# Gates and values of three head groups by Strassen's seven half products, with the weight sums made by DMA in HBM and y kept in HBM

## The chip, the core and the metric

One core of a Trainium2 chip runs the whole program once. The time is device microseconds of that execution. Its engines work side by side, each with its own queue in strict order: TensorE (PE; PEld is its loading of stationary operands), VectorE (DVE), ScalarE (ACT), GpSimd (POOL) and SyncE (SP, which here only issues DMAs). ACT and POOL can issue DMAs too. Sixteen DMA engines carry all transfers.

## What is computed

Two layers over x of 512 positions and 1024 features, in float32. Layer 0 has eight heads of retention and an RG-LRU branch; layer 1 is differential attention. After each, h = LayerNorm(sqrt 2 * h + sublayer(h)). The change is in layer 1:

```python
def odd_layer(x, w_in, ..., subln_g, w_out, pos, lambda_init):
    proj = jnp.einsum('bsd,de->bse', x, w_in)          # 1024 -> q 2048, k 2048, v 2048, g 2048
    q, k, v, g = jnp.split(proj, ...)
    q = rope(q.reshape(B, S, 2 * DIFF_HEADS, DIFF_DH), pos) * (DIFF_DH ** -0.5)
    k = rope(k.reshape(B, S, 2 * DIFF_HEADS, DIFF_DH), pos)
    out = diff_attention(q, k, v.reshape(B, S, DIFF_HEADS, DIFF_DV), lam)   # w = softmax1 - lam * softmax2, w @ v
    out = out * lax.rsqrt(jnp.mean(jnp.square(out), axis=-1, keepdims=True) + NORM_EPS) * subln_g
    out = (out * (1.0 - lambda_init)).reshape(B, S, DIFF_WIDTH) * jax.nn.silu(g)
    return jnp.einsum('bse,ed->bsd', out, w_out)
```

## The kernel before

**Numbers.** Every float32 operand of a product is split into two float32r parts, a rounded high part (a cast on ScalarE) and the rest (a subtraction on VectorE), by `split`. `mm3` makes a product of three matmuls: high by high, high by low, low by high. h, the input of layer 1, lies in SBUF as such a pair, features on partitions, 8 k tiles of 128 by 512 positions.

**Weights.** They come in blocks of 128x1024 (0.5 MB), in the order of the list `order`. `fetch` issues the load on SP's queue into one of two raw buffers and splits it into one of five pairs (`wsp`); `take(n)` hands out the next pair and has n more fetched behind it. SP and PE keep the order of the program; the other engines' instructions are put in order when the program is built, by priority.

**Units of PE.** `t_unit` makes a head's q or k (one weight block, 8 k tiles, 24 matmuls). `s_unit` makes the gates or the values of a group of two heads: 512 columns, 4 blocks of 128 positions, 4 weight blocks, each used by 24 matmuls, 96 in all; four PSUM banks of the pool `ps_pj` hold the sums. `out_unit` multiplies the mixed heads by the output weights and adds the result to y with VectorE (L239), y being 4 blocks of 128x1024 in SBUF. Layer 1 has the groups 0 to 3 (od, L262): values and gates of group 0, q and k of heads 0 to 2, then for each group its gates, its values, the output unit of two finished heads and q and k of the next two; at the end heads 6 and 7 go out, and LayerNorm and the stores follow each row block.

**Side work.** Attention is written as generators, in steps (scores; softmax; transposes; values; norm; transposes), which `Side` puts between the matmuls of the units by counting ticks (one tick is three matmuls): a new block every 8 ticks, at most three at once. Its softmax and norm run on VectorE, ScalarE and, for the inverse root, POOL. `side.need` has a step's PE instructions written before a point; `past(i - 1)` has the attention of the group before finished before its gates and values are overwritten.

**Ends.** y starts as sqrt 2 * h: the first output unit of a layer scales it while adding (L237). In the last unit of layer 1, four weight blocks (w140 to w143) are fetched at its start, with nothing ahead of them on SP but the four loads of LayerNorm's parameters:

```python
odd_out((6, 7), "oo6", after=odd_end, late=P_LAST)      # the last output unit of layer 1
w = [take(1 if n == 2 else 0) for _ in range(n)]        # out_unit: its weights
```

Of the kernel before, what the change touches and what calls it, by code (L numbers as in the profile page):

```python
# [8 lines left out]
F32 = mybir.dt.float32  # L9
# [33 lines left out]
EARLY = 2  # L43

# [51 lines left out]
def trunk(ctx: ExitStack, tc: tile.TileContext, a):  # L96
# [15 lines left out]
    small = pool("small", 4)  # L112
    ps_pj = pool("ps_pj", 4, space=PS)
# [34 lines left out]
    def mm3(out, l, r, start, stop):  # L148
        nc.tensor.matmul(out=out, lhsT=l[0], rhs=r[0], start=start, stop=False)  # L149
        nc.tensor.matmul(out=out, lhsT=l[0], rhs=r[1], start=False, stop=False)  # L150
        nc.tensor.matmul(out=out, lhsT=l[1], rhs=r[0], start=False, stop=stop)  # L151
# [67 lines left out]
    def out_unit(mix, y, name, first, before=None, after=None, late=0):  # L219
        n = len(mix)  # L220
        w = [take(1 if n == 2 else 0) for _ in range(n)]
        for sb in range(SB):
# [10 lines left out]
            for hf, ps in enumerate(pss):  # L233
                yy = y[:, sb, hf * HALF:hf * HALF + HALF]
# [30 lines left out]
    for g in range(1, 4):  # L265
        od += [("g", g), ("v", g), *[("o", (2 * g - 2, 2 * g - 1))] * (g < 3), ("qk", 2 * g + 1), *[("qk", 2 * g + 2)] * (g < 3)]
    od.append(("o", (4, 5)))
    oi = 0
    for kind, i in od:
        if kind == "o":  # L270
            order += [(oo[2 * hd + j], j) for hd in i for j in range(2)]
        else:
            order += [(ow[oi + j], None) for j in range(4)]
            oi += 4
# [257 lines left out]

    for kind, i in ev:
# [34 lines left out]
    h = pair(big, [P, KT, S], "x", "h")  # L568

    def even_end(sb):  # L570
        pts = list(layer_norm(y, sb, gb0))

        def fin():
            for hf, hv in pts:
# [77 lines left out]
    def odd_out(hds, name, **kw):  # L652
# [5 lines left out]
        out_unit([t for hd in hds for t in mix_of(om[hd])], y, name, 0 in hds, before=before, **kw)  # L658
# [13 lines left out]
    for kind, i in od:  # L672
# [16 lines left out]
        elif kind == "g":  # L689
# [6 lines left out]
            s_unit(h, f"og{i}", False, evac)  # L696
        elif kind == "qk":
# [92 lines left out]
```

## Time and profile before

| | |
|---|---|
| median of 3 runs | 942.91 us (942.73 to 943.59) |
| the profiled execution | 943.21 us, its span 941.4 us |
| PE busy, PEld busy | 923.9 us (98%), 764.8 us (81%) |
| DVE, ACT, POOL busy | 692.7 us (74%), 463.6 us (49%), 58.6 us (6%) |
| moved by DMA | 88.95 MB, all issued by SP |
| gates and values of groups 1, 2, 3 | from 534.0, 660.0 and 791 us, with attention between, 54 to 58 us each |
| last output unit | 907.4 to 932.7 us |

A row of the profile's groups gives line, engine, operation, output and inputs, shapes, count, busy time and mean duration in ns, then the idle time before and what ended it. A row of the timeline begins with start and duration in us. Matmuls overlap their neighbours: the step from one to the next is shorter than the duration shown. A row on stretches has the busy time of each engine in that stretch. The page's chain of waits has PE for 64% of the span, DVE 19%, ACT 8%.

### The profile page before, as it was taken

The numbers are of one execution on the slowest core, as the hardware profiler recorded it, in microseconds if no ns is written. First come the engines' busy times: TensorE is split into PE (matmuls) and PEld (weight loads), VectorE is DVE, ScalarE is ACT, GpSimd is POOL, SyncE is SP. The second block draws the span as 40 slices with busy tenths as digits, with TensorE's granted clock in tenths as the row PEclk, the third lists the DMA queues.
The fourth block names the chain that finished last, engine by engine and source line by source line (L and its number), as shares of the span: only waits on it lengthen the run. The fifth ranks groups of instructions, "written<-read, shape, count | busy, mean of one in ns | idle before, by whom it ended". The sixth has DMA issues, their size and how long they took to land.

```text
span 941.4 us, 11566 instructions
## 1 busy us (share of the span) xinstructions
PE 923.9 (98%) x4327; PEld 764.8 (81%) x4327; DVE 692.7 (74%) x1171; ACT 463.6 (49%) x750; POOL 58.6 (6%) x118
## 2 busy tenths in 40 slices
PE   9999999999999999999999999999999999999996
PEld 7888888878887887888887888888788888887885
DVE  5877997868779988994489854478844488636777
ACT  5567786566374776423334454233453234444340
POOL 0000000000000000000001210100100001101023
PEclk9999999999999999999999999999999999999998
DMA  6562221512314123314221222042223142223102
GB/s 225 174 218 68 90 73 54 165 57 93 120 54 148 57 90 118 120 29 162 93 89 65 69 89 90 23 134 90 68 68 90 45 135 68 73 85 113 66 23 91
DMA packets 27418, 88.95 MB, mean 94 GB/s; under 512 B 3425, under 2 KB 3553, under 8 KB 27361
## 3 DMA queue, kind: packets, MB, share of 16 engines
q1 hardware_dynamic: 27360, 88.20, 28.6%
q8 instruction: 34, 0.56, 0.2%
q14 instruction: 24, 0.19, 0.1%
HBM read 86.09 MB, written 2.10 MB: 94 GB/s over the span
## 4 chain that ended last, share of the span: by engine, by line
PE 64%; DVE 19%; ACT 8%; issue 4%; DMA 2%; POOL 2%; SPq 0%; DVEq 0%; ACTq 0%; POOLq 0%
PE ov_ps L150 3%; PE ov_ps L151 3%; PE ov_ps L149 3%; PE og_ps L149 3%; PE og_ps L150 3%; PE og_ps L151 3%; PE ev_ps L149 2%; PE ev_ps L150 2%; PE oo_ps L149 2%; PE oo_ps L150 2%; PE oo_ps L151 2%; PE ev_ps L151 2%; ACT e L610 1%; PE xb_ps L149 1%; PE xb_ps L150 1%
## 5 line engine op out<-in xcount | busy, mean ns | idle before, releaser
L610 ACT ACTIVATE e<-as,nm 128x128 f32<-128x128 f32 (+3 forms) x64 | 33.2, 523 | 29.2 <-DVE nm L607 28.8
L641 DVE SCALAR_TENSOR_TENSOR o<-po,ars,og 128x256 f32<-128x256 f32 x32 | 15.5, 484 | 39.8 <-POOL ars L326 39.8
L607 DVE CUSTOM_DVE_ANT_0 as<-as,mask 128x128 f32<-128x128 f32 (+3 forms) x64 | 30.2, 510 | 1.9 <-PE as L151 1.9
L617 POOL TENSOR_SCALAR zr<-z 128x1 f32<-128x1 f32 x32 | 11.3, 352 | 309.9 <-ACT e L610 309.9
L325 POOL TENSOR_SCALAR rs_t<-bmv 128x1 f32<-128x1 f32 x6 | 2.3, 376 | 418.4 <-DVE bmv L336 418.4
L637 ACT ACTIVATE po<-po 128x256 f32<-128x256 f32 x32 | 11.8, 370 | 29.8 <-PE po L151 25.9
L325 POOL TENSOR_SCALAR rs_t<-ss,zr 128x1 f32<-128x1 f32 x32 | 16.0, 501 | 140.5 <-ACT po L637 135.5
L239 DVE TENSOR_TENSOR y<-oo_ps,y 128x512 f32<-128x512 f32 x24 | 16.3, 684 | 4.2 <-PE oo_ps L151 4.2
L326 POOL TENSOR_TENSOR ars<-rs_t,nhalf 128x1 f32<-128x1 f32 x32 | 18.9, 591 | 2.7
L482 DVE SCALAR_TENSOR_TENSOR xc<-xbp,vecs,xc 128x509 f32<-128x509 f32 (+2 forms) x24 | 17.9, 746 | 1.5 <-ACT xc L479 1.3
L618 DVE SCALAR_TENSOR_TENSOR e<-e,zr,e 128x128 f32<-128x128 f32 (+3 forms) x32 | 17.6, 551 | 1.0
L439 DVE TENSOR_TENSOR rsd<-rs,dec 128x512 f32<-128x512 f32 (+3 forms) x32 | 15.5, 486 | 1.1 <-PE rs L151 1.0
L615 DVE RECIPROCAL zr<-z 128x1 f32<-128x1 f32 x32 | 5.2, 162 | 15.1 <-ACT e L610 14.9
L646 PEld LDWEIGHTS po<-ident,o 128*128 128x128 f32 x64 | 8.3, 140 | 7.8 <-DVE o L641 4.8
L646 PE MATMUL po<-ident,o 128*128 128x128 f32 x64 | 12.6, 278 | 1.6 <-DVE o L641 1.4
L622 PE MATMUL wt<-ident,e 128*128 128x128 f32 x80 | 14.0, 272 | 0.0
L145 ACT CAST hh<-ht 128x512 fp32r<-128x512 f32 x8 | 4.7, 588 | 18.4 <-PE ht L577 18.4
L622 PEld LDWEIGHTS wt<-ident,e 128*128 128x128 f32 x80 | 10.4, 140 | 3.8 <-DVE e L618 0.4
L498 DVE TENSOR_TENSOR xbp<-xbp,xc 128x512 f32<-128x512 f32 x8 | 5.5, 690 | 9.9 <-ACT xbp L495 9.9
L610 ACT ACTIVATION_READ_ACCUMULATOR e<-as,nm 128x1 f32 x64 | 12.5, 196 | 0.0
L504 DVE SCALAR_TENSOR_TENSOR xc<-t,r 128x512 f32<-128x512 f32 x8 | 5.5, 691 | 9.0 <-ACT r L503 9.0
L408 ACT ACT_TABLE_LOAD x9 | 11.5, 1283 | 0.8 <-PE gl_ps L151 0.7
(2673 smaller groups left out, 3416.3 us busy)
## 6 DMA issues: line engine op xcount, KB each, us to landing
w_r<-in_od_w SPq DMA_DIRECT2D x64, 512.0 KB, 3.3
w_r<-in_ev_w SPq DMA_DIRECT2D x47, 512.0 KB, 3.3
w_r<-in_ev_wo SPq DMA_DIRECT2D x16, 512.0 KB, 3.4
w_r<-in_od_wo SPq DMA_DIRECT2D x16, 512.0 KB, 3.3
dec<-in_dec SPq DMA_DIRECT2D x8, 256.0 KB, 3.9
y<-in_x SPq DMA_DIRECT2D x4, 512.0 KB, 6.8
out_h<-y SPq DMA_DIRECT2D x8, 256.0 KB, 2.1
xr<-in_xt SPq DMA_DIRECT2D x3, 512.0 KB, 6.7
```

The lines of the kernel that those rows point to most:

```text
L149: nc.tensor.matmul(out=out, lhsT=l[0], rhs=r[0], start=start, stop=False)
L150: nc.tensor.matmul(out=out, lhsT=l[0], rhs=r[1], start=False, stop=False)
L151: nc.tensor.matmul(out=out, lhsT=l[1], rhs=r[0], start=False, stop=stop)
L239: nc.vector.tensor_tensor(out=yy, in0=ps, in1=yy, op=ALU.add)
L325: nc.gpsimd.tensor_scalar(out=t, in0=var, scalar1=scale, scalar2=eps, op0=ALU.mult, op1=ALU.add)
L326: nc.gpsimd.tensor_tensor(out=out, in0=t, in1=nhalf[:, :1], op=ALU.pow)
L482: nc.vector.scalar_tensor_tensor(out=xc[:, sh:], in0=xb[:, :S - sh], scalar=conv_w(w, c), in1=xc[:, sh:], op0=ALU.mult, op1=ALU.add)
L607: nc.vector.tensor_tensor_reduce(out=ps[:, :n], in0=ps[:, :n], in1=mask[:, S - n:], scale=-QK_SCALE, scalar=3.0e38, op0=ALU.add, op1=ALU.m ...
L610: nc.scalar.activation(out=e, in_=ps[:, :n], func=AF.Exp, scale=-1.0, bias=nm, accum_out=z[:, mp:mp + 1])
L618: nc.vector.scalar_tensor_tensor(out=ee[0], in0=ee[1], scalar=zr[:, 0:1], in1=ee[0], op0=ALU.mult, op1=ALU.add)
L622: nc.tensor.transpose(out=pt[:, kb * P:kb * P + P], in_=ee[0][:, kb * P:kb * P + P], identity=ident)
L646: nc.tensor.transpose(out=pm[:, i * P:i * P + P], in_=o[:, i * P:i * P + P], identity=ident)
```

## The change

1. **Gates and values of groups 1 to 3 are one unit, `gates_values`.** h is cut into halves of positions (r) and of features (c), the weights into two halves of features and gates against values. Seven products of such blocks replace eight: a product takes two weight blocks and makes two row blocks of 128x512 in 24 matmuls. Of the seven left factors three are plain blocks of h and four are sums; of the seven right ones three are plain weights and four are sums. Results are combined with copies on ScalarE and additions on VectorE; two pairs of `ps_pj` banks are used in turn. A weight block serves 12 matmuls, and a group takes 14 blocks where it took 8.
2. **The weight sums, `weight_sums`,** 24 blocks of 0.5 MB in HBM, are made by POOL's DMA queue: a copy from the weights and an accumulating transfer for each, 48 transfers of 0.5 MB. In the program they are side work from tick 30 on, 10 ticks apart.
3. **The sums of h, `act_sums`,** are made by VectorE behind the gates of group 0, in `st`, which takes y's place in SBUF; four pairs of 1 MB are stored to HBM by POOL's queue, and ACT's queue loads them into `sx` two at a time (`load_sum`, 2 DMAs of 0.5 MB each, eight per group).
4. **y in HBM.** After the even layer ScalarE scales h by sqrt 2 and POOL's queue stores it to `yd`. The first three output units copy their banks on ScalarE and POOL's queue adds them to `yd` (24 accumulating transfers of 256 KB). Before the last unit SP loads y again, 4 blocks of 0.5 MB.

```diff
+    sums = []
...
+        elif kind == "gv":
+            b = {(r, c): [ow[oi + 4 * c + 2 * r + j] for j in range(2)] for r in range(2) for c in range(2)}
+            t = {n: [dram.tile([P, D], F32, tag=f"t{i}{n}{j}", name=f"t{i}{n}{j}") for j in range(2)] for n in (1, 2, 3, 4)}
+            for j in range(2):
+                for n, one, two in ((1, b[0, 1], b[0, 0]), (3, b[1, 1], b[0, 1]), (2, b[1, 1], t[1]), (4, b[1, 0], t[2])):
+                    sums += [(t[n][j], one[j], None), (t[n][j], two[j], ALU.add)]
+            for n in (b[0, 0], b[1, 0], t[2], t[3], t[1], t[4], b[1, 1]):
+                order += [(n[j], None) for j in range(2)]
...
+    def weight_sums():
+        for dst, src, op in sums:
+            nc.gpsimd.dma_start(out=dst, in_=src, max_dma_last_dim=4 * D, **({"accum_op": op} if op else {}))
+            yield SUM_GAP
...
+    side.add(weight_sums(), "sums", 1, SUM_START)
...
+                nc.scalar.activation(out=hv, in_=hv, func=AF.Identity, scale=ALPHA)
+                nc.gpsimd.dma_start(out=yd[sb][:, hf * HALF:hf * HALF + HALF], in_=hv)
...
+    def add_to_y(sb, hf, ps):
+        t = work(f"oy{sb}{hf}")
+        nc.scalar.copy(out=t, in_=ps)
+        nc.gpsimd.dma_start(out=yd[sb][:, hf * HALF:hf * HALF + HALF], in_=t, accum_op=ALU.add)
...
+        def put(k, n):
+            split(lows[k], (st[:, k, 0].bitcast(F32R), st[:, k, 1].bitcast(F32R)))
+            nc.gpsimd.dma_start(out=sd[n], in_=st[:, k])
...
+        st = big.tile([P, 2, 2, KT // 2, 2 * P], F32, tag="y", name="st")
+        lows = [st[:, k, 1] for k in range(2)]
+        difference(lows[0], (1, 1), (1, 0))
+        add(lows[1], 0, 0, ALU.subtract, less(lows[1], lows[0]))
+        put(0, 0)
+        add(lows[0], 0, 1, ALU.subtract, less(lows[0], lows[1]))
+        put(1, 1)
+        put(0, 3)
+        difference(lows[1], (0, 0), (1, 0))
+        put(1, 2)
...
+    def load_sum(n, k):
+        for j in range(2):
+            nc.scalar.dma_start(out=sx[:, k, :, 2 * j:2 * j + 2].bitcast(F32), in_=sd[n][:, :, 2 * j:2 * j + 2])
...
+        def product(ps, left, start):
+            for j in range(2):
+                w = take(2)
+                for n in range(2):
+                    for kt in range(2 * j, 2 * j + 2):
+                        c = kt % 2 * HALF
+                        mm3(ps[n], left(kt, n), cut(w, ALL, slice(c, c + HALF)), start and kt == 0, kt == KT // 2 - 1, skip_group_check=not start)
+                        side.tick()
...
+        product(one, block(0, 0), True)
+        p1 = copies(one, "p1")
+        product(two, block(0, 1), True)
+        gate(two, p1, 0)
+        product(one, total(0), False)
+        u = copies(one, "u")
+        load_sum(0, 0)
+        product(two, total(1), True)
+        p7 = copies(two, "p7")
+        load_sum(3, 1)
+        product(one, total(0), False)
+        past(i - 1)
+        low = []
+        for n in range(2):
+            nc.vector.scalar_tensor_tensor(out=p7[n], in0=one[n], scalar=-1.0, in1=p7[n], op0=ALU.mult, op1=ALU.subtract)
+            low.append(pair(vp, [P, S], "v", f"ov{i}{2 + n}"))
+            split(p7[n], low[n])
+        product(two, block(1, 1), False)
+        gate(two, u, 1)
+        product(one, total(1), False)
...
-            odd_out(i, f"oo{i[0]}")
+            odd_out(i, f"oo{i[0]}", keep=add_to_y)
     gb1 = ln_params(a["od_ln"], "ln1", *((qkp, n) for n in ("qh", "ql", "kh", "kl")))
+    y = big.tile([P, SB, D], F32, tag="y", name="y2")
+    for sb in range(SB):
+        nc.sync.dma_start(out=y[:, sb], in_=yd[sb])
     odd_out((6, 7), "oo6", after=odd_end, late=P_LAST)
```

How the order of instructions changes, at three places. First POOL's queue at the start of the program. Before, the first instructions behind the memset are those of the LayerNorm after the even layer:

```order
L302 MEMSET nhalf_158 128x4
L325 ISA
L325 TENSOR_SCALAR rs_t_3412<-bmv_3409 128x1 [waits DVE_49]
L326 TENSOR_TENSOR lrs_3411<-rs_t_3412,nhalf_158 128x1 [waits Pool_49]
```

Now (t110 is a weight sum in HBM: group 1, sum 1, block 0; DMASW is a counter of landed POOL transfers):

```order
L320 MEMSET nhalf_184 128x4
L386 DMA t110_101<-in_od_w 128x1024
L386 DMA t130_105<-in_od_w 128x1024
L386 DMA t120_103<-in_od_w 128x1024
L386 DMA t110_101<-in_od_w 128x1024 [waits DMASW0_49]
L386 DMA t130_105<-in_od_w 128x1024 [waits DMASW1_49]
L386 DMA t140_107<-in_od_w 128x1024
L386 DMA t120_103<-t110_101 128x1024 [waits DMASW3_49,DMASW2_49]
L386 DMA t111_102<-in_od_w 128x1024
```

The 48 transfers stand in one row before LayerNorm's first instruction, and none of them waits for another engine: the ticks set their place in the order, nothing more. Second, VectorE in the gate stage of group 0 (ov02 and ov03 are values of group 0, which PE's banks hold until then; w68 to w71 the weights of that stage), before:

```order
L146 TENSOR_TENSOR w68l_3767<-w68_r_3765,w68h_3766 128x1024 [waits DMAHW6_49,Activation_49]
L146 TENSOR_TENSOR w69l_3773<-w69_r_3771,w69h_3772 128x1024 [waits DMAHW7_49,Activation_49]
L146 TENSOR_TENSOR ov02l_3720<-ov0_ps2_3694,ov02h_3719 128x512 [waits Activation_49]
L146 TENSOR_TENSOR w70l_3779<-w70_r_3777,w70h_3778 128x1024 [waits DMAHW0_49,Activation_49]
L146 TENSOR_TENSOR w71l_3809<-w71_r_3807,w71h_3808 128x1024 [waits DMAHW1_49,Activation_49]
L146 TENSOR_TENSOR ov03l_3749<-ov0_ps3_3723,ov03h_3748 128x512 [waits Activation_49]
```

and now:

```order
L149 TENSOR_TENSOR w69l_3871<-w69_r_3869,w69h_3870 128x1024 [waits DMAHW7_49,Activation_49]
L714 TENSOR_TENSOR st_4003<-hh_3431 128x1024 [waits DMASW4_49,DMASW5_49,DMASW3_49,DMASW6_49,DMASW2_49,DMASW7_49,DMASW1_49,DMASW0_49]
L715 TENSOR_TENSOR st_4003<-st_4003,hl_3432 128x1024 [waits DVE_49]
L149 TENSOR_TENSOR ov02l_3818<-ov0_ps2_3792,ov02h_3817 128x512 [waits Activation_49]
L716 TENSOR_TENSOR st_4003<-st_4003,hl_3432 128x1024 [waits DVE_49]
L149 TENSOR_TENSOR w70l_3877<-w70_r_3875,w70h_3876 128x1024 [waits DMAHW0_49,Activation_49]
L707 SCALAR_TENSOR_TENSOR st_4003<-st_4003,hh_3431 128x1024 [waits DVE_49]
L149 TENSOR_TENSOR w71l_3907<-w71_r_3905,w71h_3906 128x1024 [waits DMAHW1_49,Activation_49]
L149 TENSOR_TENSOR ov03l_3847<-ov0_ps3_3821,ov03h_3846 128x512 [waits Activation_49]
```

Sums of h stand between; the first of them waits until y has been stored. Third, SP's queue around the last output unit, whose weights are w140 to w143 before and w158 to w161 now. Before:

```order
L155 DMA ln110_7993<-in_od_ln 128x512
L155 DMA ln111_7995<-in_od_ln 128x512
L171 DMA w140_r_7997<-in_od_wo 128x1024 [waits DMAHW4_49,DVE_49]
L171 DMA w141_r_8003<-in_od_wo 128x1024 [waits DMAHW5_49,DVE_49]
L171 DMA w142_r_8009<-in_od_wo 128x1024 [waits DMAHW2_49,DVE_49]
L171 DMA w143_r_8015<-in_od_wo 128x1024 [waits DMAHW3_49,DVE_49]
```

Now:

```order
L158 DMA ln111_8267<-in_od_ln 128x512
L851 DMA y2_8269<-yd0_3433 128x1024 [waits DMASW4_49,DMASW5_49,DMASW3_49,DMASW6_49,DMASW2_49,DMASW7_49,DMASW1_49,DMASW0_49]
L851 DMA y2_8269<-yd1_3434 128x1024 [waits DMASW7_49,DMASW6_49]
L851 DMA y2_8269<-yd2_3435 128x1024 [waits DMAHW6_49,DMASW1_49,DMASW0_49]
L851 DMA y2_8269<-yd3_3436 128x1024 [waits DMAHW7_49,DMASW3_49,DMASW2_49]
L174 DMA w158_r_8274<-in_od_wo 128x1024 [waits DMAHW0_49,DVE_49,Activation_49]
L174 DMA w159_r_8280<-in_od_wo 128x1024 [waits DMAHW1_49,DVE_49]
L174 DMA w160_r_8286<-in_od_wo 128x1024 [waits DMAHW2_49,DMAHW0_49,DVE_49]
L174 DMA w161_r_8292<-in_od_wo 128x1024 [waits DMAHW3_49,DMAHW1_49,DVE_49]
```

The four loads of y stand ahead of the weights, each waiting for the sums that POOL's queue adds to its block; the last two of those sums are the end of the third output unit.

More of the change, by code (lines that the diff above doesn't have):

```diff
@@ L43 @@
 EARLY = 2
+SUM_START, SUM_GAP = 30, 10
 class Side:
@@ L112, in trunk @@
     small = pool("small", 4)
+    dram = pool("dram", 1, space=bass.MemoryType.DRAM)
     ps_pj = pool("ps_pj", 4, space=PS)
@@ L217, in s_unit, with out_unit @@
                     product(ps[sb], w, sb, 2 * i + j)
-    def out_unit(mix, y, name, first, before=None, after=None, late=0):
+    def out_unit(mix, y, name, first, before=None, after=None, late=0, keep=None):
         n = len(mix)
@@ L568, in trunk @@
     h = pair(big, [P, KT, S], "x", "h")
+    yd = [dram.tile([P, D], F32, tag=f"yd{sb}", name=f"yd{sb}") for sb in range(SB)]
     def even_end(sb):
```

68 lines of the change are left out of this document (62 added, 6 removed).

## The prediction

> **What bounds the kernel now.** I read the busy shares first, then the stages, then PE's waits, then the last 60 us instruction by instruction. From the page, the busy times:
>
> ```profile
> PE 923.9 (98%) x4327; PEld 764.8 (81%) x4327; DVE 692.7 (74%) x1171; ACT 463.6 (49%) x750; POOL 58.6 (6%) x118
> ```
>
> A busy PE need not be a PE that sets the time, so the stages (start:end, length, then the busy time of PE, PEld, DVE, ACT and POOL with counts in brackets, PE's clock, DMA share, GB/s):
>
> ```profile
> 5.00:10.00 5.00, 4.95 (x11) 3.64 (x12) 2.16 (x5) 1.94 (x5) 0.00 (x0) 1.00 0.89 324
> 10.00:15.00 5.00, 5.00 (x22) 4.07 (x22) 3.68 (x5) 2.65 (x5) 0.00 (x0) 1.00 0.87 258
> 15.00:20.00 5.00, 5.00 (x24) 4.14 (x23) 3.70 (x12) 3.30 (x6) 0.00 (x0) 1.00 0.84 304
> 20.00:25.00 5.00, 5.00 (x24) 4.13 (x23) 4.54 (x18) 1.31 (x2) 0.00 (x0) 1.00 0.01 2
> ...
> 300.00:400.00 100.00, 98.15 (x450) 81.22 (x450) 88.40 (x139) 62.77 (x85) 2.17 (x2) 1.00 0.29 96
> ...
> 433.00:454.50 21.50, 21.50 (x96) 17.81 (x95) 6.73 (x6) 8.71 (x10) 0.00 (x0) 1.00 0.44 147
> 454.50:534.00 79.50, 78.42 (x382) 64.68 (x381) 65.38 (x122) 31.83 (x68) 9.20 (x16) 1.00 0.24 79
> 534.00:588.20 54.20, 54.20 (x271) 45.59 (x270) 30.55 (x65) 29.05 (x57) 5.23 (x11) 1.00 0.24 79
> ...
> 907.00:933.00 26.00, 25.81 (x128) 21.39 (x126) 23.07 (x44) 5.41 (x13) 7.03 (x11) 1.00 0.13 47
> 933.00:941.40 8.40, 0.00 (x0) 0.00 (x0) 5.29 (x8) 0.17 (x1) 3.48 (x3) 0.66 0.32 126
> ```
>
> In every stretch from 5 us to 933 us PE is filled but for 1 or 2%, and the head of its list of waits is small (total, times, longest):
>
> ```profile
> PE po L646 <- DVE o L641: 1.4, 3, 0.5
> PE po L149 <- DVE om6l L146: 1.1, 3, 0.7
> ```
>
> So the time is PE's work, a start of about 5 us and 8.4 us of the last LayerNorm. A matmul taken away anywhere pays in full, and a wait put on PE anywhere costs in full. The DMA engines are a quarter to a third busy in the long stretches, but 0.84 to 0.89 between 5 and 20 us, when x and the first weights arrive.
>
> **What the change takes away.** Gates and values of groups 1 to 3 were 192 matmuls of 128x512 per group (two products, 4 row blocks, 8 k tiles, 3 terms); now a group has seven half products of 24, 168 in all. One matmul's step comes from the starts of two weight tiles in the gate stage of group 0:
>
> ```profile
> L149 PE MATMUL og_ps<-w68h,hh x8: 389/389/389, 433.0 to 437.7; 128*128 128x512 f32 x8
> L149 PE MATMUL og_ps<-w69h,hh x8: 389/389/389, 438.4 to 443.2; 128*128 128x512 f32 x8
> ```
>
> (438.4 - 433.0) / 24 = 0.226 us (the 389 ns overlap their neighbours). 3 x 24 x 0.226 = **-16.3 us**. The 24 additions of y on VectorE go too (16.3 us, 684 ns each), but PE was not waiting for them, so I count nothing.
>
> **The start: the sums of weights.** The Python spaces these 48 transfers out, but they are on POOL's queue and wait for one another alone; the first three go out right behind the memset of nhalf. They carry 0.5 MB each and so meet the loads that use 0.84 to 0.89 of the DMA engines. What PE needs by then:
>
> ```profile
> 19.21 1.05 ACT L145 CAST w3h<-w_r 128x1024 fp32r<-128x1024 f32 x1 [1.24 <-DMA w_r<-in_ev_w]
> 22.96 1.22 DVE L146 TENSOR_TENSOR w3l<-w_r,w3h 128x1024 fp32r<-128x1024 f32 x1
> ...
> L150 PE MATMUL ev_ps<-w3l,xh x8: 389/389/395, 24.5 to 29.2; 128*128 128x512 f32 x8
> ```
>
> w3 lands at 19.2 us, and with its two halves of splitting (1.05 + 1.22) could be ready 3 us ahead of 24.5. If the sums took half of the engines, the 17 us of loading at 0.87 become 17 x 0.87/0.5 = 29.6, w3 would land at 31.8 and PE be 9.6 us late (31.8 + 2.3 - 24.5). If they took a quarter, 17 x 0.87/0.75 = 19.7, landing at 21.9, nothing. The bounds are 0 and 9.6; three copies at a time, with a wait for landing in between, lie between a quarter and a half: **+5**. The Trainium skill (DMA: Bandwidth & Descriptors, Queues, rings and completion order) has each DMA engine take turns between the queues that have work, packet by packet. By that rule the half applies and the sum below is 4.6 us higher; no run so far shows two busy queues. Later weights are split well ahead of their use (w12 at 57.8, used from 76.7), and that lead hides the rest of the sums; uncovered, each load of the even layer would be late by what it lost.
>
> ```profile
> 57.79 1.22 DVE L146 TENSOR_TENSOR w12l<-w_r,w12h 128x1024 fp32r<-128x1024 f32 x1
> ...
> L151 PE MATMUL q_ps<-xh,w12l x8: 389/389/393, 76.7 to 83.1; 128*128 128x512 f32 x8
> ```
>
> **The sums of h.** VectorE gets 14 instructions of 128x1024, about 1.23 us each as w3l above: 17.2 us. The gate stage of group 0 has 21.5 - 6.7 = 14.8 us free. Two of the 14 wait for a 1 MB store of st, and rows of weights and the evacuation ov03l queue behind them. In the next stage VectorE is at 65.4 of 79.5, and PE lost 1.1 us there. Bounds 0 and 6.6 (17.2 - 14.8 = 2.4, and two stores at 2.1 us, which the out_h row further down has for 256 KB); I take **+1.5**, since most of the 14 find a free engine.
>
> **The seven products.** A weight tile now serves 12 matmuls, so a group splits 14 tiles for 8. Added on VectorE: 6 x 1.23 + 6 x 0.69 (four gate sums, two for the value half) = 11.5; on ScalarE 6 x 1.05 + 6 copies x 0.58 + 8 DMA issues x 0.33 + a second switch to Silu and back, 2 x 1.28, = 15.0.
>
> ```profile
> L477 ACT COPY xbp<-xb_ps 128x512 f32<-128x512 f32 x8 | 4.6, 579 | 1.3 <-PE xb_ps L151 1.3
> L693 ACT ACT_TABLE_LOAD x5 | 6.4, 1283 | 0.1
> L239 DVE TENSOR_TENSOR y<-oo_ps,y 128x512 f32<-128x512 f32 x24 | 16.3, 684 | 4.2 <-PE oo_ps L151 4.2
> ```
>
> Group 1's stage (534 to 588) shrinks to 48.8 us; VectorE has 42.0 of it (86%), ScalarE 44.1 (90%). The stages with VectorE at 82% and 88% above lost 1.1 of 79.5 and 1.9 of 100 us of PE: 2% of 146 us is 3. The last product's two banks are the first that the next unit takes; their evacuation (0.58 + 0.69 and the hops) is 0.3 to 1 us longer than the 1.36 us of matmuls that cover it: 2 in three groups. **+5**; bounds 2 and 15 (a third of ScalarE's 15 us per group not covered).
>
> **POOL in the out units.** 24 accumulating transfers stand among the steps of attention that VectorE waits for:
>
> ```profile
> L641 DVE SCALAR_TENSOR_TENSOR o<-po,ars,og 128x256 f32<-128x256 f32 x32 | 15.5, 484 | 39.8 <-POOL ars L326 39.8
> ```
>
> At SP's 0.33 to 0.43 us an issue, 24 are 9 us, most of it beside POOL's idle time; **+1.5**, bounds 0 and 6.
>
> **The end: y comes back in front of the last weights.** SP's queue now has the four loads of y before w158 to w161, and the last of them waits until the last sum of the third out unit has landed in HBM. Before, w140 to w143 had only buffers to wait for:
>
> ```profile
> 905.78 0.39 PE L151 MATMUL oo_ps<-w139h,om5l 128*128 128x512 f32 x1
> 907.38 0.39 PE L149 MATMUL oo_ps<-w140h,om6h 128*128 128x512 f32 x1
> 912.11 0.39 PE L150 MATMUL oo_ps<-w143l,om7h 128*128 128x512 f32 x1
> ...
> 908.13 1.15 ACT L142 ACTIVATE w143h<-w_r,sg 128x1024 fp32r<-128x1024 f32 x1 [2.14 <-DMA w_r<-in_od_wo]
> 909.32 1.28 DVE L143 SCALAR_TENSOR_TENSOR w143l<-w_r,sg,w143h 128x1024 fp32r<-128x1024 f32 x1 [0.18 <-ACT w143h L142]
> ...
> w_r<-in_od_wo SPq DMA_DIRECT2D x16, 512.0 KB, 3.3
> ln<-in_ev_ln SPq DMA_DIRECT2D x4, 256.0 KB, 3.7
> out_h<-y SPq DMA_DIRECT2D x8, 256.0 KB, 2.1
> ```
>
> In the clock of the profile before: the third out unit's last matmul is over at 906.0; copy 0.6; issue 0.4; the 256 KB sum, which no row shows, between a store alone (2.1) and a load and a store (3.7 + 2.1 = 5.8), taken as 4.0; two issues 0.7; w158 3.3, and 0.8 for the y block ahead of it (half of the 1.6 us that 0.5 MB take at the 324 GB/s above); first half of the split 1.15: 916.9, where PE started at 907.38. Two raw buffers hold only w158 and w159, so w160 starts when w158 is split (918.2) and w161 1.3 us later: 919.5 + 0.3 + 3.3 + 1.15 + 1.28 = 925.5 for the matmul that ran at 912.11. **+13.4**, bounds 11 and 16 (by the 2.1 and 5.8, and the 0.8 from 0 to 1.6). PE has 25.8 of the 26 us after 907 filled, so nothing gives it back. The Trainium skill (DMA: Bandwidth & Descriptors, Anatomy of one DMA) fits a transfer issued by GpSimd with 2.0 us + bytes/436e3, 2.6 us here. By that the sum below would be 1.4 us lower.
>
> The four layers of y that ScalarE scales after the even layer (8 x 0.6 us) fall where it has most of its time free (14.1 of 40 us busy from 400 to 440), at no cost; uncovered they would be 5 us.
>
> ```profile
> 400.00:440.00 40.00, 40.00 (x193) 33.16 (x192) 29.57 (x44) 14.07 (x19) 2.23 (x6) 1.00 0.29 87
> ```
>
> **The sum.** -16.3 + 5 + 1.5 + 5 + 1.5 + 13.4 = +10.1. The profiled execution took 943.2 us (span 941.4 and 1.8 around it), 0.3 over the median of 942.9: 943.2 + 10.1 = 953.3, or **953**.
>
> **The rivals.** (a) *Faster: the transfers inside HBM only take what the loads leave.* Then the start costs nothing, and with the vector engines' and POOL's lower bounds 943.2 - 16.3 + 11 + 0 + 2 = 940. For it: after 20 us the engines stand idle (2 GB/s from 20 to 25 us), and a sum waits for its copy. Against: from 5 to 20 us there is little left to take. It decides as long as w3 lands before 22 us and the gate and value stages lose under 1 us each. (b) *The sums hold half of the engines all through the start*: 953.3 + 4.6 = 958. For it the three copies in flight; against it, each sum waits until its copy has landed, and loads fill the gap. The rule of the Trainium skill named above would have it so. (c) *ScalarE becomes the bound of the three gate and value stages.* At 90% with strict order, and issues that wait for PE, a third of the added work lands on PE: 953.3 + 10 = 963. For it: attention's exp, the copies that free PE's banks and the weight splits stand in one queue. Against: 88% on VectorE cost only 2%. (d) *The change doesn't do what it says*: the last unit's weights would be there before y; then the end costs nothing and the time is 940. SP's order speaks against it.
>
> **How the numbers follow.** The forecast 0.42, (a) 0.16, (b) 0.14, (c) 0.22, (d) 0.06. The forecast's own range is 946 to 958. The range that takes in (a), (d) and most of (c) is 938 to 970; about one in ten lies on either side. A measurement of this kernel tells 0.2% (1.9 us) from no change: faster is (a) and (d) less what falls within, 0.20; same 0.05; slower 0.75.
>
> **What would show it.** Right: some 72 fewer matmuls; w3's split around 29 us in place of 23; PE idle for about 10 us before the first matmul of the last out unit, with SP waiting for a y store; the gate and value stages some 3 to 4 us shorter instead of 5.4, ScalarE near 90% there. Wrong: no idle time at the end (SP's wait is short), first weights as early as now, or PE waits of several us in the three stages.

## The result, and the profile after

The changed kernel takes **1027.07 us** (median of 4 runs, 1024.92 to 1029.9) against 942.84 us for the kernel before beside it (942.73 to 943.59): a ratio of 1.0893 (95% interval 1.0862 to 1.0924). Slower was forecast, but by 10 us, and it is 84. The time lies far outside the range. Each run of the next section was executed once; the four runs of the changed kernel lie within 5.0 us of one another, those of the kernel before within 0.9.

The page of the changed kernel, busy times, and PE's clock and the DMA share in 40 slices:

```profile
PE 937.8 (91%) x4255; PEld 760.9 (74%) x4255; DVE 724.6 (71%) x1197; ACT 517.6 (50%) x829; POOL 122.4 (12%) x202
...
PEclk9889898999999999999999999999998999999978
DMA  9999962141322322324661247662365642454542
```

PE has exactly 72 fewer matmuls recorded, and yet more busy time, since part of it runs at a lower granted clock. The first five slices of 25.7 us show DMA engines that are full. By stretches (columns as in the prediction):

```profile
0.00:50.00 50.00, 40.57 (x133) 29.73 (x134) 23.14 (x56) 15.78 (x23) 12.55 (x23) 0.90 0.97 303
50.00:100.00 50.00, 40.80 (x166) 32.01 (x164) 26.08 (x34) 21.19 (x26) 10.86 (x16) 0.93 1.04 317
100.00:150.00 50.00, 43.30 (x188) 35.77 (x188) 38.76 (x58) 33.75 (x46) 9.75 (x14) 0.90 0.89 237
150.00:200.00 50.00, 44.75 (x192) 36.49 (x193) 37.01 (x58) 34.13 (x47) 0.00 (x0) 0.93 0.21 69
```

By the clock column (last but two) these 200 us lose at most (0.10 + 0.07 + 0.10 + 0.07) x 50 = 17 us of full-clock work to a slower clock, an estimate; w24 starts 44 us later than before (184.7 instead of 140.9 us), so the greater part of the delay is waiting.

The head of PE's waits (total, times, longest), where before nothing was over 1.4 us:

```profile
PE oo_ps L152 <- ACT w158h L145: 10.5, 1, 10.5
PE rs L152 <- DVE rsd L462: 9.8, 3, 8.8
PE wt L649 <- DVE e L645: 7.3, 4, 3.3
PE pr L152 <- ACT xc0h L148: 5.9, 1, 5.9
PE oo_ps L152 <- ACT w126h L145: 3.9, 1, 3.9
PE ev_ps L152 <- ACT w3h L148: 3.1, 1, 3.1
PE pr L152 <- ACT xc2h L148: 2.9, 1, 2.9
```

To see where the time went I took, in each trace, the start of the first matmul on the first weight tile of each stage, and from these the length of the stage (us). "Front" is from the odd layer's first matmul to the stage of group 1. The last four columns are runs of the next section.

| stage | before | changed | difference | no sums, y late | seven blocks | no reloads | no adds |
|---|---|---|---|---|---|---|---|
| first layer | 409.2 | 458.9 | +49.7 | 409.4 | 409.5 | 409.6 | 409.7 |
| front | 124.8 | 129.2 | +4.4 | 127.9 | 128.0 | 130.7 | 128.0 |
| gates and values 1 | 54.4 | 51.9 | -2.5 | 51.1 | 48.7 | 48.7 | 51.1 |
| out unit 0 | 29.3 | 32.8 | +3.5 | 33.2 | 29.9 | 29.9 | 33.5 |
| heads 3, 4 | 47.8 | 49.7 | +1.9 | 49.2 | 50.0 | 49.5 | 47.9 |
| gates and values 2 | 53.3 | 52.1 | -1.2 | 52.3 | 49.0 | 49.3 | 52.4 |
| out unit 2 | 29.3 | 41.8 | +12.5 | 39.9 | 29.9 | 31.6 | 39.3 |
| heads 5, 6 | 47.8 | 49.3 | +1.5 | 49.1 | 49.2 | 49.2 | 47.8 |
| gates and values 3 | 53.3 | 52.1 | -1.2 | 51.2 | 48.9 | 49.3 | 50.9 |
| head 7 | 30.2 | 31.0 | +0.8 | 30.8 | 30.3 | 34.5 | 30.9 |
| out units 4 and 6, end | 62.0 | 77.9 | +15.9 | 62.2 | 62.0 | 62.0 | 62.1 |
| span | 941.4 | 1026.7 | +85.3 | 956.3 | 935.4 | 944.3 | 953.6 |

The stages of groups 2 and 3 of the kernel before start at 665.5 and 795.9 us and take 53.3 us each; the table ahead of the prediction starts them some 5 us too early. Three places hold nearly all of the difference: the first layer (+49.7), the second out unit (+12.5) and the end (+15.9).

### The profile page after: what moved, and what is told of

It reads as the page before. It is cut to its first block, busy times and chain, and to the rows that moved or that the text cites. A ratio compares the mean times of both kernels' runs of the same rounds, so it can differ in the third digit from the quotient of the medians.

```text
span 1026.7 us, 11812 instructions
## 1 busy us (share of the span) xinstructions
PE 937.8 (91%) x4255; PEld 760.9 (74%) x4255; DVE 724.6 (71%) x1197; ACT 517.6 (50%) x829; POOL 122.4 (12%) x202
## 4 chain that ended last, share of the span: by engine, by line
PE 18%; DVE 14%; DMA 8%; ACT 5%; issue 4%; POOL 2%; ACTq 0%; DVEq 0%; SPq 0%; POOLq 0%
DMA w_r<-in_od_w 2%; DMA w_r<-in_od_wo 2%; PE oo_ps L153 2%; DMA w_r<-t 2%; PE oo_ps L154 2%; PE oo_ps L152 2%; ACT e L637 1%; DMA sd<-st 1%; POOL ars L344 1%; POOL rs_t L343 1%; PE po L152 1%; ACT L637 1%; PE po L154 1%; PE po L153 1%; PE wt L649 1%
## 5 line engine op out<-in xcount | busy, mean ns | idle before, releaser
L668 DVE SCALAR_TENSOR_TENSOR o<-po,ars,og 128x256 f32<-128x256 f32 x32 | 15.5, 484 | 40.2 <-POOL ars L344 39.3
L644 POOL TENSOR_SCALAR zr<-z 128x1 f32<-128x1 f32 x32 | 14.9, 467 | 231.4 <-ACT e L637 231.2
L690 POOL DMA_DIRECT2D yd<-oy x24 | 21.6, 903 | 62.4 <-ACT oy L689 49.3
L343 POOL TENSOR_SCALAR rs_t<-ss,zr 128x1 f32<-128x1 f32 x32 | 13.9, 435 | 119.8 <-ACT po L664 110.2
L386 POOL DMA_DIRECT2D t<-in_od_w x36 | 24.4, 725 | 31.1 <-DMA t<-in_od_w 21.1
L689 ACT COPY oy<-oo_ps 128x512 f32<-128x512 f32 x24 | 14.1, 588 | 20.6 <-PE oo_ps L154 18.2
L642 DVE RECIPROCAL zr<-z 128x1 f32<-128x1 f32 x32 | 5.2, 163 | 24.2 <-ACT e L637 23.9
L386 POOL DMA_DIRECT2D t<-t x12 | 10.0, 830 | 77.2 <-DMA t<-in_od_w 47.4
```

The costliest lines, as they stand in the source:

```text
L343: nc.gpsimd.tensor_scalar(out=t, in0=var, scalar1=scale, scalar2=eps, op0=ALU.mult, op1=ALU.add)
L386: nc.gpsimd.dma_start(out=dst, in_=src, max_dma_last_dim=4 * D, **({"accum_op": op} if op else {}))
L690: nc.gpsimd.dma_start(out=yd[sb][:, hf * HALF:hf * HALF + HALF], in_=t, accum_op=ALU.add)
```

## Experiments

### The sums: left out, alone, and half of them

The theory is S: the sums, all under way at once, starve the loads of the first layer. Its first rival, R, has other parts of the change delay that layer. The sums left out of the changed kernel:

```
-            for n in (b[0, 0], b[1, 0], t[2], t[3], t[1], t[4], b[1, 1]):
+            for n in (b[0, 0], b[1, 0], b[1, 1], b[0, 1], b[0, 1], b[1, 0], b[1, 1]):
...
-    side.add(weight_sums(), "sums", 1, SUM_START)
```

> The 48 sum transfers are left out, and the seven products read 14 unsummed blocks per group in the same order and number (so gates and values are not the reference's; every other instruction stands). Theory S, the sums starve the first loads: in the changed kernel they keep the 16 DMA engines at 0.93 to 1.06 from 10 to 120 us, and 23 weights of 512 KB land in 7.5 us (median) where 31 did in 3.3. Then w24 starts at 141 to 146 us as in the kernel before (140.9) and not at 184.7, the odd layer (w64) at 411 to 418 and not at 458.9, and the whole is 978 to 988 us. Rival R, the rest of the change (other orders on VectorE and ScalarE, y kept in HBM) causes the delay of the first layer: w24 stays above 165 and the whole above 1005 us.

975.96 us, a little below the range of S; w24 starts at 139.9 and w64 at 407.8 us, even earlier than S said. S holds, and R falls. The odd layer still takes 566 us against 532. The opposite edit, the kernel before with the same 48 transfers and nothing that reads them:

```
+    side.add(weight_sums(), "sums", 1, 30)      # in the kernel before
```

> The kernel before, with the same 48 transfers added on GpSimd's queue and nothing that reads what they make: the disputed cost by itself. Theory S: w24 starts at 178 to 188 us instead of 140.9 and the whole is 942.8 + 44 to 50 = 985 to 994 us. The prediction's own step (start +5, the rest hidden by weights split ahead): 945 to 952 us. Rival R: 943 to 955 us too, so R and the prediction's step fall together here if it is above 980.

990.99 us, +47.5; w24 starts at 182.7. So the disputed cost is some 48 us by itself, and the prediction's 5 is refuted. Half of the transfers, the copies alone:

```
-        for dst, src, op in sums:
+        for dst, src, op in sums[::2]:
```

> The kernel before with 24 of the 48 transfers of the earlier run, the plain copies alone (12.6 MB in place of 25.2; that run took 991.0 us). If bytes moved decide, half of its 47.5 us: 964 to 969 us. If an adding transfer, which reads its target too, costs twice a copy, a third: 956 to 961 us. If only the first 30 us are hurt, as the prediction had it, 945 to 952 us.

967.58 us, +24.6, inside the range for "bytes decide". I don't take it as a law, because the time on the DMA engines does not follow the bytes. The queue's rows of this run (0 to 70 us) and of the changed kernel (0 to 190 us) give megabytes and share:

```profile
q0 software_dynamic: 3456, 12.58, 47.5%
```

```profile
q0 software_dynamic: 6912, 25.17, 51.4%
...
t<-in_od_w POOLq DMA_DIRECT2D x36, 512.0 KB, 10.5
w_r<-in_ev_w SPq DMA_DIRECT2D x23, 512.0 KB, 7.5
```

24 copies hold 0.475 x 70 = 33 us of all 16 engines, 1.4 us each; all 48 hold 0.514 x 190 = 98 us, so an adding transfer comes to (98 - 33) / 24 = 2.7 us, twice a copy, if the copies take the same in both runs. The copies alone cost the kernel 24.6 us, and the adding transfers 22.9 more (47.5 - 24.6), with twice the engine time. The copies hit the start hardest: with them alone w4 starts at 45.8 us, with all 48 at 40.8, before at 29.7. The last row is what reaches PE: a weight block lands in 7.5 us, where the kernel before has, for the same stretch:

```profile
w_r<-in_ev_w SPq DMA_DIRECT2D x31, 512.0 KB, 3.3
```

### Paced

Now each transfer waits for the TensorE instruction ahead of it in the program, which is the spacing that the Python only hints at:

```
+    def after_pe(ins):   # ins waits for the last TensorE instruction emitted so far
-            nc.gpsimd.dma_start(out=dst, in_=src, ...)
+            after_pe(nc.gpsimd.dma_start(out=dst, in_=src, ...))
```

> Each of the 48 sum transfers also waits for the TensorE instruction that stands ahead of it in the program, one transfer per 10 steps of three matmuls (some 6.8 us), from step 30 on; bytes and results as before. Theory S, what costs is that they all run at once: spread over 30 to 370 us they ask 512 KB per 6.8 us = 77 GB/s beside the weights' 512 KB per 5.4 us = 97 GB/s, a transfer lands in 3 to 6 us, w24 starts at 141 to 148 us, the whole is 978 to 990 us. Rival Q, what costs is their engine time (51.4% of 190 us = 98 us of all 16 engines), whenever it is spent: the same 40 to 50 us of delay, spread over the first 370 us, the whole 1010 to 1027 us.

1002.61 us, w64 at 436.2: between the two theories, and a miss for both. Pacing gives back 23 of the 51 us that the first layer loses against the run without sums; 28 stay, though the engines are far from full (0 to 436.2 us):

```profile
q1 hardware_dynamic: 14544, 44.94, 29.8%
q0 software_dynamic: 7072, 25.69, 26.5%
...
w_r<-in_ev_w SPq DMA_DIRECT2D x47, 512.0 KB, 4.4
```

The sums' queue, with 0.5 MB of y in it, holds 0.265 x 436 = 116 us of engine time here, more than the 98 above, so the time per transfer is no constant. At a share of 56% (29.8 + 26.5) a weight block lands in 4.4 us instead of 3.3, and PE's longest waits in this layer are not for weights themselves (30 to 436 us):

```profile
PE rs L152 <- ACT k5h L148: 3.4, 1, 3.4
PE ro_ps L152 <- DVE gl L436: 3.3, 1, 3.3
PE rs L152 <- ACT k3h L148: 2.7, 1, 2.7
PE ht L606 <- DVE y L376: 2.6, 1, 2.6
```

Wider spacing:

```
-SUM_START, SUM_GAP = 30, 10
+SUM_START, SUM_GAP = 30, 18
```

> The paced run with one sum transfer per 18 steps in place of 10: about 30 of the 48 fall into the first layer, the rest into the odd one. If each transfer costs what it did (27 us for 48 = 0.56 us), the odd layer starts at 409 + 30 x 0.56 = 424 to 428 us and the whole stays at 997 to 1006 us. If it is only transfers that overlap with one another or with bursts of weights that cost, the odd layer starts at 412 to 420 us and the whole is 980 to 994 us.

1004.26 us, the first case by the total; w64 at 421.5 us lies between the two. 28 transfers lie in the first layer and cost 13.7 us there (421.5 - 407.8), the others cost the odd layer 16 us (581 us from w64 on, against 565). Spreading them moves the cost, it does not remove it.

### By which way a sum transfer reaches PE

The trace of the changed kernel shows a way that the prediction did not have. ScalarE and VectorE in the largest wait, and TensorE:

```profile
100.24 1.04 ACT L148 CAST w14h<-w_r 128x1024 fp32r<-128x1024 f32 x1 [10.34 <-DMA w_r<-in_ev_w]
...
101.31 1.23 DVE L149 TENSOR_TENSOR w14l<-w_r,w14h 128x1024 fp32r<-128x1024 f32 x1 [9.66 <-ACT w14h L148]
...
105.69 0.68 DVE L462 TENSOR_TENSOR rsd<-rs,dec 128x512 f32<-128x512 f32 x1
...
106.43 0.58 PE L152 MATMUL rs<-q0h,k0h 128*128 128x256 f32 x1 [8.79 <-DVE rsd L462]
107.67 0.63 PE L153 MATMUL gr_ps<-xl,w11h 128*128 128x512 f32 x1
108.09 0.63 PE L154 MATMUL gr_ps<-xh,w11l 128*128 128x512 f32 x1
...
L154 PE MATMUL gl_ps<-xh,w14l x8: 389/389/395, 126.9 to 131.7; 128*128 128x512 f32 x8
```

w14 is split 25 us before PE uses it, so for its own matmuls it is not late at all. But its cast and its subtraction stand in two queues that run in order, and what stands behind them, rsd, is what PE needs next. A lead in time does not cover a wait in a queue. The other long waits are of this kind (xc0h stands behind the cast w9h, which waits 5.2 us for its block), and between 45 and 459 us PE waits for a weight's own split only once, 0.3 us for w63l. In the paced run it is the same with w50h, which waits for its block, and k5h behind it:

```profile
312.75 1.04 ACT L148 CAST w50h<-w_r 128x1024 fp32r<-128x1024 f32 x1 [5.68 <-DMA w_r<-in_ev_wo]
313.70 0.61 ACT L148 CAST k5h<-k_c 128x512 fp32r<-128x512 f32 x1
```

A first attempt to show it by a run set the split one unit ahead instead of two, with and without sums:

```
+        ins = nc.scalar.copy(out=dst[0], in_=src)   # the cast of a block
+        if hold[0]:             # first layer, blocks fetched two units ahead
+            after_pe(ins)
...
```

> The paced run (1002.6 us; the odd layer starts at 436.2 us where the kernel before has 409.2) with one more edit, in the first layer alone: a weight block that is fetched two units ahead is split one unit ahead, and ScalarE's cast waits for TensorE to get there, so that the cast stands behind, not ahead of, the casts of q, k and scores that TensorE waits for next. Theory H, the 27 us come from ScalarE's queue (a cast that waits for a late block holds up what stands behind it, as at k5h, where w50h waits 5.7 us and PE then 3.4): against its own control (next run) the odd layer starts at most 12 us later. Theory Q, engine time taken by the sums itself delays blocks that are needed: 20 to 30 us later, as now.

> The control of the run before: the same later split in the kernel without the sums (975.96 us, odd layer at 407.8). If a split one unit ahead is early enough, the odd layer starts at 406 to 413 us and the whole is 974 to 982 us. If it is too late by itself, the odd layer starts later than 415, and the pair says less.

1024.21 and 1005.45 us, w64 at 458.4 and 439.7. The control lost 32 us up to w64 by itself: a split one unit ahead (24 matmuls, 5.4 us) is too late for these queues. The difference of 18.7 us fits neither theory and the pair decides nothing.

The second attempt takes the weight loads away, not the splits:

```
+            again = 8 <= n < 60      # then split again what lies in the buffer since w7
+            raw = kept[0] if again else wraw.tile([P, D], F32, tag="raw", name=f"w{n}_r")
...
+                if not again:
+                    nc.sync.dma_start(out=raw[:, c], in_=src[:, c])
```

> Control of the next two: the run without the sums (975.96 us, odd layer at 407.8 us), in which the 52 weight blocks w8 to w59 of the first layer are not loaded: each is split again from the block that lies in the raw buffer since w7, by the same instructions (the first layer's values are wrong). All theories: odd layer at 404 to 409 us, the whole 972 to 978 us.

> The same in the paced run (1002.6 us, odd layer at 436.2 us). Theory C, a paced sum transfer costs 0.56 us because a weight block lands later beside it (4.4 us instead of 3.3) and its cast holds up ScalarE's and VectorE's queues: with no weight block to land, the odd layer starts at most 6 us after the control's. Theory P, the transfers cost by another way (GpSimd building their descriptors beside VectorE's work, or memory shared with all engines): still 18 to 30 us after the control's.

> The same in the changed kernel itself (1027.1 us, odd layer at 458.9 us). Theory C: what is left of its 50 us are the loads up to w7, cos, sin, vecs, gw, dec and x, which stay: w8 starts at about 75 us as now (22.7 us late), and after it little is added, odd layer at 430 to 440 us. Theory P: odd layer at 450 to 459 us.

979.28, 990.98 and 999.19 us; the control is 1.3 us above its range. What the sums cost by these points (start of w24, w52 and w64 against the control without sums, us):

| | w24 | w52 | w64 |
|---|---|---|---|
| all at once, with loads | +44.8 | +47.2 | +51.1 |
| all at once, w8 to w59 not loaded | +14.2 | +15.1 | +18.6 |
| paced, with loads | +6.2 | +18.7 | +28.4 |
| paced, w8 to w59 not loaded | +2.4 | +4.9 | +15.1 |

C holds in the main. With the sums at once, 30.6 of the 44.8 us up to w24 go when there are no blocks to wait for, and of the 14.2 left 13.3 are there at w8 already (66.5 against 53.2 us): the start (w8 came at 66.5 and not at the 75 expected, since its own block was no longer waited for). Paced, 13.8 of the 18.7 us up to w52 go. With the sums at once the odd layer starts at 429.0 us, just below C's 430 to 440 and far from P's. Leaving out the loads also takes their share of the engines away, so these runs show that it is the late blocks, and the waits in the traces above that they act through the queues. By its letter the paced number was missed by both: 15.1 us at w64, where C said 6 at most and P 18 to 30. Its last 10 us fall behind w52, where the blocks from w60 on are loaded again. Two waits of PE stand there:

```profile
PE ht L610 <- DVE y L380: 3.4, 1, 3.4
PE ro_ps L152 <- DVE gl L440: 3.0, 1, 3.0
```

gl stands behind w61l on VectorE, whose cast waited for its block: the way of C. The transpose waits for the LayerNorm, and GpSimd's queue, first of this run and then of its control, tells why:

```profile
404.78 1.04 POOL L347 TENSOR_SCALAR rs_t<-bmv 128x1 f32<-128x1 f32 x1 [0.54 <-DVE bmv L358]
413.33 0.75 POOL L347 TENSOR_SCALAR rs_t<-bmv 128x1 f32<-128x1 f32 x1 [7.51 <-DVE bmv L358]
414.15 1.48 POOL L348 TENSOR_TENSOR lrs<-rs_t,nhalf 128x1 f32<-128x1 f32 x2
```

```profile
396.68 0.74 POOL L343 TENSOR_SCALAR rs_t<-bmv 128x1 f32<-128x1 f32 x1 [395.86 <-DVE bmv L354]
397.50 0.55 POOL L344 TENSOR_TENSOR lrs<-rs_t,nhalf 128x1 f32<-128x1 f32 x1
```

With paced transfers in that queue, the second row block's rs_t has been put ahead of the first one's lrs, which then waits 7.5 us for a row block that comes later. That is an order which came with the pacing, and no cost of the transfers themselves. How much of the last 10 us each of the two takes I have not separated, and P is not excluded for the rest of them.

### The end

```
+    while len(ready) < len(order):
+        list(fetch())
     for sb in range(SB):
         nc.sync.dma_start(out=y[:, sb], in_=yd[sb])
```

> The changed kernel with one edit: the last four weights (w158 to w161) are fetched on SyncE's queue ahead of the four loads of y, not behind them. Theory Y, the wait of 10.5 us for w158 in the last-but-one unit is the queue's order: it goes, the unit oo4 to oo6 takes 28 to 31 us instead of 38.6, the whole 1014 to 1019 us. Rival Z, y then comes too late for the last unit's sums: the wait moves to the last unit, which takes 45 us or more instead of 39.3, and the whole stays at 1022 to 1030 us.

1015.14 us. SyncE's queue in the changed kernel and in this run:

```profile
960.10 21.44 SPq L851 DMA_DIRECT2D y<-yd  x4
981.64 8.72 SPq L174 DMA_DIRECT2D w_r<-in_od_wo  x4
```

```profile
949.61 27.15 SPq L174 DMA_DIRECT2D w_r<-in_od_wo  x3
977.07 11.58 SPq L853 DMA_DIRECT2D y<-yd  x4
```

From w154 to the end it takes 62.2 us (77.9 in the changed kernel, 62.0 before). Theory Y holds, and y is in time. The total falls by 12 and not by 16, because this run reached w64 5 us later than the other. Without sums as well:

> Both large losses taken out: the run without the sums (975.96 us) with the last four weights fetched ahead of the loads of y (it too computes other gates and values than the reference). If the two add up, the stretch from w154 to the end takes 62 us as in the kernel before and not 78.6, and the whole is 975.96 - 16.5 = 958 to 962 us. If the wait at the end only showed because of the sums, it is 965 to 976 us. It is the base of the next three.

958.09 us, w154 to the end 62.2: the two add up. With the paced sums, the best that keeps the result:

> The two mends that keep the result, together: paced sums and the last four weights ahead of the loads of y. The end costs 16 us by unit (62 us from w154 on instead of 78): 1002.6 - 16 to 17 = 984 to 988 us, still 41 to 45 us above the kernel before.

986.04 us, as expected, and 43 us above the kernel before. No run with the right result beats the kernel before.

### The stages of gates and values

All three runs are based on the one without sums and with y late (958.09 us). One block for two in each half product:

```
-            for j in range(2):
-                w = take(2)
+            w = take(2)
+            for j in range(2):
```

> As the base of this call, but each half product reads one block of 512 KB twice in place of two blocks: 7 loads and splits per group instead of 14, and the same 168 matmuls (the values are wrong by this too). Theory W, the half products use up a block in 12 matmuls (2.7 us) where the kernel before used 24 (5.4 us), and load plus split with two raw buffers cannot keep that rate: the stages of gates and values fall from 50.6, 53.1 and 51.5 us to 47 to 49.5, the out unit behind the second falls from 39.6 to 30 to 34 us, the whole to 938 to 948 us. Rival E, what stands behind the products (copies, sums and splits on ScalarE and VectorE, the reloads of sums) limits: the stages stay within 1 us each, the whole at 955 to 962 us.

The sums of h loaded once:

```
-        load_sum(0, 0)   # and the other three of each group
```

> As the base of this call, but the sums of the layer's input are loaded once and never again (20 loads of 512 KB on ScalarE's queue left out; the products then read the wrong sums). Theory W: within 3 us of the base, since PE waits for weights. Theory X, these loads (5 us each to land) hold up weight loads and ScalarE's queue: the out unit behind the second stage falls from 39.6 to 30 to 35 us and the whole by 6 to 14 us.

Out units that drop their results:

```
-            odd_out(i, f"oo{i[0]}", keep=add_to_y)
+            odd_out(i, f"oo{i[0]}", keep=lambda *_: None)
```

> As the base of this call, but the first three out units drop their results (no copy on ScalarE, no adding transfer of 256 KB on GpSimd's queue; 24 of each left out). Theory O, these 24 transfers on the queue on which the attention's small GpSimd work stands are what lengthens the out units (33.7 and 39.6 us against 29.3 before): both at 29 to 31 us, the whole 10 to 16 us below the base. Theory W: the first falls by at most 2 us, the second stays above 36 us because weights come late there, the whole 1 to 4 us below the base.

937.22, 946.03 and 955.42 us; by stage they are the last three columns of the table above. W is confirmed by the first (the total is 0.8 us below its range): the stages fall by 2.4, 3.3 and 2.3 us, and the out units behind two of them to 29.9 us. This run leaves out half of the casts and subtractions too, so by itself it can't tell the loads from the work of ScalarE and VectorE. But X is confirmed by the second as well: the stages fall by 2.4, 3.0 and 1.9 us, the out units to 29.9 and 31.6. Each removal nearly suffices, so it is the two together that are too much: W's claim that the reloads matter by 3 us at most falls. The second run has all casts and subtractions and settles the prediction's rival (c). Stage 1 of the base, then without reloads:

```profile
537.30:588.40 51.10, 49.19 (x248) 41.01 (x247) 38.06 (x75) 34.67 (x67) 6.23 (x11) 1.00 0.55 183
```

```profile
540.30:589.00 48.70, 48.70 (x247) 41.17 (x245) 39.21 (x76) 35.82 (x68) 5.05 (x11) 1.00 0.41 132
```

With ScalarE and VectorE as busy as in the base, PE has no gap. Whether the reloads act through the DMA engines or through ScalarE's queue, in which their issues stand, is not shown. A raw buffer is held from the issue to the end of the subtraction. The time to landing of the weight blocks around group 2 (min, median, max) in the base and without reloads:

```profile
DMA to landing us min/median/max: 3.2/3.5/6.5
```

```profile
DMA to landing us min/median/max: 3.2/3.3/5.1
```

0.33 to issue, 3.3 to land, 1.05 to cast and 1.23 to subtract are 5.9 us, for two buffers 3.0 us a block; a half product uses a block in 12 x 0.226 = 2.7 us. With attention between, the stage has 51.1 / 14 = 3.65 us a block, and a landing of 6.5 us, beside reloads that take 5.2 themselves, breaks it: (0.33 + 6.5 + 1.05 + 1.23) / 2 = 4.6, an estimate. The stage eats the lead, and the out unit, which needs four blocks at once, pays: between 670.8 and 763 us PE waits in the base for seven splits of weights, 0.3 to 1.7 us each, and without reloads for one (668.4 to 749 us). These waits also cost clock. Out unit 2 of the base:

```profile
723.10:763.00 39.90, 34.72 (x146) 26.66 (x146) 15.98 (x25) 17.82 (x33) 9.22 (x16) 0.87 0.58 134
```

0.13 x 39.9 = 5 us at most of the 10.6 by which it is longer than before are the slower clock.

O is refuted: the out units stay at 33.5 and 39.3 us. The copies on ScalarE and the adding transfers, which this run leaves out together, cost 1.3 us in each of the two stretches of heads behind them (49.2 and 49.1 to 47.9 and 47.8), 2.7 us in all. The run without reloads lost 2.8 us in the front and 3.7 in head 7; the cause is open.

## Why the prediction was wrong

- **The failed step** is the sentence on later weights in "The start: the sums of weights": that they are split well ahead of their use and "that lead hides the rest of the sums". Measured, the sums cost 47.5 us alone and 49.7 in the first layer, where 5 stood. Two things are wrong in it. No engine time was worked out: the 48 transfers hold all DMA engines for 98 us, and no lead of 19 us (57.8 to 76.7) outlasts that. A block of 0.5 MB at the 324 GB/s of a row that I had quoted is 1.6 us; 48 such transfers are 77 us even if an adding one cost no more than a copy. And a lead is no cover where the waiting split stands ahead of urgent work in ScalarE's and VectorE's queues (w14, 25 us ahead, and an 8.8 us wait).
- **The start itself** is at the upper bound of 9.6 or above, and not 5: PE reaches w3h at 33.9 us instead of 24.2 and w3l, by which the bound was worked out, at 35.8 instead of 24.5, 11.3 late. At w8 it is 22.7 (75.5 instead of 52.8). Between 2 and 20 us the two queues hold half of the engines each:

```profile
q0 software_dynamic: 722, 2.66, 53.1%
q1 hardware_dynamic: 1139, 3.14, 46.5%
```

This is rival (b) for the start. The trace agrees with the turn-taking between queues that the Trainium skill states (DMA: Bandwidth & Descriptors, Queues, rings and completion order). I had taken the middle of two bounds, against a rule that gave the upper one.
- **Fewer matmuls** (-16.3) came, and were eaten: gates and values fall by 4.9 us in all, and two out units rise by 16.0, together +11.1 where -16.3 + 5 = -11.3 was forecast. The term "seven products" is mis-sized, 27 instead of 5, above its bound of 15. I had counted ScalarE's and VectorE's work, as in rival (c), and not the rate of the blocks: 14 loads in a stage instead of 8, beside 4 MB of reloads. Rival (c) did not decide: I had ScalarE at 44.1 us of stage 1 (90%), and its row in the base has 34.67 of 51.1 (68%). Taking half of the blocks away brought 20.9 us (958.1 to 937.2), 13.3 of them in the out units.
- **The sums of h**: the front is 4.4 us longer, where 1.5 stood with bounds 0 and 6.6. The gate stage, in which most of them run, takes 0.7 us of it (22.4 instead of 21.7), the heads behind it 3.7, with one wait of PE of 3.3 us for e on VectorE. No run leaves these sums out, so it is not shown that they cause it.
- **POOL**: 2.7 us by the run that drops copies and adds, inside 0 to 6, but in the heads behind the out units. An issue took 0.90 us and not 0.33 to 0.43, so the 24 hold POOL for 21.6 us instead of 9:

```profile
L690 POOL DMA_DIRECT2D yd<-oy x24 | 21.6, 903 | 62.4 <-ACT oy L689 49.3
```

- **The end** was right in mechanism, place and bounds: 15.9 us for 13.4 (11 to 16). A sum of 256 KB landed in 4.5 us, where I took 4.0, and where the fit of the Trainium skill (DMA: Bandwidth & Descriptors, Anatomy of one DMA) gave 2.6:

```profile
yd<-oy POOLq DMA_DIRECT2D x24, 256.0 KB, 4.5
```

- **The copies that scale y** cost nothing that can be seen: they run from 458.6 us on, and the stretch from w64 to w68 takes 23.8 us as before (458.9 to 482.7 against 409.2 to 433.0).

By the table, 49.7 + 4.4 + 11.1 + 4.2 (the three stretches of heads) + 15.9 = 85.3. Of the sum's six terms the removed matmuls came, three stayed inside their bounds (the sums of h with a cause not shown), and the two that failed, by 44.7 and 22 us, are the same kind of omission: the traffic of weight blocks was never compared with what two raw buffers and the shared engines can bring.

## What to carry to other kernels

Before work is moved to DMA "beside" a full TensorE, multiply it out in engine time (transfers x share x time) and set it against the idle share of that stretch; then ask what a slower landing holds up in the in-order queues that split or cast what lands, not only whether the block itself is in time. A product with fewer matmuls that uses each block half as long doubles the rate of loads, casts and buffer turns; what it saves on TensorE has to be set against that rate. And a load that waits for a store belongs behind the loads that wait for nothing.

## What the runs showed of the hardware

- An adding transfer of 512 KB inside HBM holds the 16 engines for about 2.7 us, a copy for 1.4: an estimate from the shares of two runs (33 us for 24 copies, 98 us for all 48).
- A wait costs TensorE more than its length. After the 8.8 us wait shown above the step is 108.09 - 107.67 = 0.42 us instead of 0.226 until 112 us, some 2.6 us more. The stretches there have the granted clock at 1.00, 0.50 and 1.00, and behind a wait of 2.9 us (xc2h) at 0.51:

```profile
97.60:101.70 4.10, 0.04 (x1) 0.00 (x0) 0.39 (x1) 1.45 (x2) 0.85 (x1) 1.00 1.05 317
101.70:112.00 10.30, 5.57 (x15) 4.51 (x16) 9.24 (x14) 5.47 (x9) 2.39 (x4) 0.50 1.02 254
112.00:115.00 3.00, 3.00 (x16) 2.54 (x15) 2.51 (x4) 2.30 (x4) 0.00 (x0) 1.00 1.03 415
...
152.90:159.80 6.90, 5.96 (x15) 4.61 (x15) 4.34 (x7) 3.90 (x5) 0.00 (x0) 0.51 0.46 152
```

PE stopped at 97.6 and began again at 106.4 us: the half clock came some 4 us into the wait and stayed for 5.6 us of work. The Trainium skill (TensorE: Matmul & The Clock Gate, What's actually happening) states a half clock after an idle window of some 3.4 us and the full one after as long a busy window, with windows that run freely. The trace agrees with the half; a wait of 2.9 us was enough here, and the full clock came later than 3.4 us after the first matmul, for which windows that do not begin with the work leave room.
- A weight block of 512 KB landed in 3.3 us in the kernel before, in 4.4 beside the paced sums (engines at a share of 56%) and in 7.5 beside the sums all at once (engines full).
